# Sums of rows on TensorE, the last expert kept on chip, and products to fill a gap: one change to a transformer block with a mixture of experts

## The chip, the cores and the metric

The kernel runs on one core of one Trainium2 chip. Its time is the device time of one execution in microseconds; the median of three runs is given. TensorE (PE in the profile) multiplies matrices into PSUM, VectorE (DVE), ScalarE (ACT) and GpSimd (POOL) work on tiles of 128 partitions, and SyncE (SP) issues most of the transfers between HBM and the chip. TensorE's clock is granted by the chip; the profile shows it as a share of full speed (2.4 GHz), and its other level is half of that (1.2 GHz).

## The reference, cut to what matters

The reference is one transformer block on 1024 tokens of width 1024. After attention and a first normalization, every token is routed to 2 of 32 experts, and the results are added and normalized:

```python
t = h.reshape(B * S, D)                                   # 1024 x 1024
g_prob = softmax(t @ w_rg + b_rg)                         # 4 groups, the best one
e_top, e_idx = top_k(e_in_group, 2)                       # 2 of its 8 experts
e_w = softmax(e_top) * g_w
for e in range(32):
    hid = silu(t @ w1[e]) * (t @ w3[e])                   # 1024 -> 256
    y = y + gate[:, e:e + 1] * (hid @ w2[e])              # 256 -> 1024
...
x = layer_norm(DN_ALPHA * x + gt2[:, None, :] * f, ln2_g, ln2_b)   # f is y
```

All of it is f32.

## The kernel before, in words

The kernel does attention first; the change starts where the first normalization is done and the tokens are routed. Eight tiles of 128 tokens are taken through `products`, `residual`, `first_norm`, `second_norm`, `transposed`, `logits`, `choose` (which experts), `place` (which slot of the expert) and `slots`. VectorE does the small operations of the routing in order, tile by tile; the last tile, 7, goes through the shorter `fast_first` and `fast_second`. `slot_rows` then turns the slots into row numbers, `gather_x` fetches the first three experts' rows from HBM into `xg`, `weigh` and `slot_weights` work out the gates.

In the expert loop (`for e in range(NE)`) each expert has up to 128 slots. Its rows are transposed (`expert_x`, tile `etp`), multiplied with the gate and up weights into `eph` (`expert_up`), passed through silu and the gate (`expert_act`, tile `esg`), transposed again (`expert_h`, `ehp`) and multiplied with the down weights (`expert_down`, tile `ey`). A product of f32 values is done as three single-pass products, of high and low parts: `split` makes a weight's high part on ScalarE (`ehi`) and the low part on VectorE (`elo`). For the very first expert the low parts are held back (`hold=True`) and made later by `low_parts`. Weights come in pages of 1 MB; `page` hands the pages of three pools out in turn, and a load waits until its page has been split. `scatter_y` writes an expert's rows to `dy` in HBM by their row numbers: each token has two rows there, one for each of its experts, 1024 rows apart.

After the loop comes a branch: if some expert had more than 128 tokens (`nblk > 0`), a block for the overflow runs. It is skipped in the profiled execution. Then the last phase: for each of eight tiles of 128 tokens the two rows are loaded from `dy` (`rr`, `r2s`), added, multiplied with `gt2`, added to the kept residual `xa`, normalized and written out. Its order is written by hand in the string `LAST`: a letter is a step, a digit the tile. On TensorE a sum is made by multiplying with the identity (`summed`): a and b add the two rows, x and z add the residual. On VectorE b is an addition, g the product with `gt2`, s and o the scaling and shifting, and m a fused addition for the tiles of `FDX`. Else m, the mean, is on ScalarE, and so is most of v, the variance; v ends with two small operations on GpSimd.

The orders of TensorE, VectorE, ScalarE and GpSimd are as the code is written; each engine works its list off in order. SyncE's list is set by a scheduler.

Of the kernel before, what the change touches and what calls it, by code (L numbers as in the profile page):

```python
# [10 lines left out]
F32 = mybir.dt.float32  # L11
# [4 lines left out]
AF = mybir.ActivationFunctionType  # L16
# [30 lines left out]
FDX = (0, 7)  # L47
FPS = (3, 5)
# [36 lines left out]
x1 x2 x3 x4 b0 g0 m0 b1 v0 g1 s0 z1 b2 m1 o0 v1 a3 g2 s1 z2 b4 b3 m2 o1 v2 a5 g4 g3 z4 s2 z3 m4 b6  # L85
o2 v4 b5 g6 m3 x5 s4 v3 g5 x6 o4 z5 s3 b7 z6 m5 o3 v5 g7 m6 s5 v6 m7 o5 v7 s6 s7 o6 o7
# [72 lines left out]
def block_kernel(ctx, tc, A, out, dbg=None, stop=99):  # L159
# [1134 lines left out]
    GP.memset(ones, 1.0)  # L1294
    gat = rtp.tile([128, 2, NT], F32, name="gat")
# [45 lines left out]
    def weigh(t):  # L1341

        L, g8, m8 = (rt[t].pop(n) for n in ("L", "g8", "m8"))
        ng_ = rtw.tile([128, 4], F32, name="rng")
        V.tensor_tensor(ng_[:, 0:1], m8[:, 1:2], m8[:, 0:1], op=OP.subtract)
        V.tensor_tensor(L[:, :4], L[:, :4], g8[:, 0:1].to_broadcast([128, 4]), op=OP.subtract)
        SC.activation(L[:, :4], L[:, :4], AF.Exp, accum_out=ng_[:, 1:2])
        SC.activation(ng_[:, 0:1], ng_[:, 0:1], AF.Exp)
        V.scalar_tensor_tensor(ng_[:, 2:3], ng_[:, 0:1], 1.0, ng_[:, 1:2], op0=OP.add, op1=OP.mult)
        V.reciprocal(gat[:, 0, t:t + 1], ng_[:, 2:3])  # L1350
        V.tensor_tensor(gat[:, 1, t:t + 1], gat[:, 0, t:t + 1], ng_[:, 0:1], op=OP.mult)
# [277 lines left out]
    place(t - 2)  # L1629
    transposed(t)  # L1630
# [10 lines left out]
    slots(t)  # L1641
    keep(t, z)
# [53 lines left out]
    def expert_down(xpool, pp, W2, Hs):  # L1696
        y = xpool.tile([128, D], F32, name="ey", bufs=NEY)
        for half in range(2):
            ps = pp.tile([128, 512], F32, name="eyp", bufs=2)
            cs = slice(half * 512, half * 512 + 512)  # L1700
            for k in range(2):
                mm3(ps, Hs[0][:, k], Hs[1][:, k], *(x[:, cs] for x in W2[k]), k == 0, k == 1)
            SC.activation(y[:, cs], ps, AF.Copy)
        return y
# [61 lines left out]

    with tc.tile_pool(name="ex", bufs=2) as ex, tc.tile_pool(name="epp", bufs=1, space=PSUM) as epp:
# [3 lines left out]
        low_parts(2)  # L1771
# [4 lines left out]
        def down(e):  # L1776
            return expert_down(ex, epp, W.pop((e, 2)), Hs)
# [7 lines left out]
        for e in range(NE):  # L1785
# [25 lines left out]
        scatter(down(NE - 1), NE - 1)  # L1811
# [5 lines left out]
    with tc.If(nblk > 0):  # L1817
        with tc.tile_pool(name="otp", bufs=1, space=PSUM) as otp:
            overflow_tables(otp.tile([128, 512], F32, name="osums"))
        with tc.For_i(0, nblk) as b:  # L1820
            with tc.tile_pool(name="ow", bufs=1) as ow, tc.tile_pool(name="opp", bufs=1, space=PSUM) as opp:
                ve = nc.values_load(blk[0:1, bass.ds(b, 1)], min_val=0, max_val=NE - 1)
                Wo = [split(fetch(ve, i, pg), i) for i in range(3)]
                cols = wr[:, 7, :2].bitcast(I32)
                gc = wr[:, 7, 2:3]
                V.tensor_copy(cols[:, 0:1], gidx[:, bass.ds(b + NE, 1)])
                V.tensor_copy(cols[:, 1:2], sidx[:, bass.ds(b + NE, 1)])
                V.tensor_copy(gc, gsl[:, bass.ds(b + NE, 1)])
                gather_x(xg[0], cols[:, 0:1])
                *_, Xo = expert_x(ow, opp, xg[0])  # L1830
                ph = expert_up(opp, Wo, Xo)
                scatter_y(expert_down(ow, opp, Wo[2], expert_h(es2, opp, expert_act(es2, ph, gc))), cols[:, 1:2])


    ews.close()
    with tc.tile_pool(name="fin", bufs=NT) as fp, tc.tile_pool(name="fpp", bufs=4, space=PSUM) as fpp:
        rr, r2s = [], []
        for t in range(NT):
            for rows_, o, n in ((rr, 0, NT), (r2s, S, NT)):
                rows_.append(fp.tile([128, D], F32, name=f"fr{o}", bufs=n))  # L1840
                SY.dma_start(rows_[t], dy[o + t * 128:o + (t + 1) * 128])  # L1841
# [3 lines left out]
        def summed(t, j, x, first):  # L1845

            if first:
                fs[t, j] = fpp.tile([128, D], F32, name="fps")
            for half in range(2):
                sl = slice(half * 512, half * 512 + 512)  # L1850
                PE.matmul(fs[t, j][:, sl], ident, x[:, sl], start=first, stop=not first)  # L1851

        def added(t):
            V.tensor_tensor(rr[t], rr[t], r2s[t], op=OP.add)

        def gated(t):
            V.tensor_tensor(rr[t], fs.pop((t, 0)) if t in FPS else rr[t], gt2, op=OP.mult)

# [18 lines left out]
        def shift(t):  # L1877
# [48 lines left out]
```

## Time and profile before

| | us |
|---|---|
| median of 3 runs | 1409.38 (1406.3 to 1409.62) |
| the profiled execution | 1403.06 |
| its span, first to last instruction | 1401.3 |
| mean granted clock over the span | 0.967 |
| TensorE busy | 1308.8 (93%) |
| VectorE busy | 1145.8 (82%) |
| ScalarE busy | 717.4 (51%) |
| GpSimd busy | 440.5 (31%) |

The span is a little less than the program's time; the rest lies before the first and after the last instruction. The shares are averages over stages with different limits. The expert loop at its steady pace lies between 1055 and 1340, the last phase takes the last 57 us.

### The profile page before, as it was taken

How to read it: one execution, taken by the hardware profiler on the slowest of the kernel's cores; microseconds unless marked ns; L12 is line 12 of the kernel's file. 1: busy time of each engine (PE TensorE's matmuls, PEld its weight loads, DVE VectorE, ACT ScalarE, POOL GpSimd, SP SyncE). 2: the span in 40 equal slices, each digit the busy share in tenths (PEclk: the TensorE clock that was granted, in tenths of full speed). 3: DMA queues.
4: the chain of work that ended last, by engine and by line, in shares of the span. 5: the costliest groups of instructions: out<-in, count | busy, mean ns of one | idle time of the engine just before them, and what ended most of it. 6: DMA issues, size and time to landing. Idle time of an engine off the chain costs nothing. (4 is left out here: it accounts for less than half of the span.)

```text
span 1401.3 us, 21266 instructions
## 1 busy us (share of the span) xinstructions
PE 1308.8 (93%) x7535; PEld 1057.7 (75%) x7535; DVE 1145.8 (82%) x2137; ACT 717.4 (51%) x1306; POOL 440.5 (31%) x474
## 2 busy tenths in 40 slices
PE   4989999999999999998989999999779999999965
PEld 2568888887888788985557778999758888888832
DVE  5738888887988899974788749788889999999947
ACT  1546765444244321323665644222248888889824
POOL 2422123375237521232544425211212222222114
PEclk9999999999999999999999999999869999999987
DMA  8475422112211223103864458745469999999954
GB/s 285 158 210 183 138 78 76 43 56 73 72 61 39 74 87 106 61 31 122 318 230 138 137 152 261 273 168 209 151 214 374 372 381 371 373 348 363 375 224 177
DMA packets 133998, 264.91 MB, mean 189 GB/s; under 512 B 20736, under 2 KB 71224, under 8 KB 131840
## 3 DMA queue, kind: packets, MB, share of 16 engines
q1 hardware_dynamic: 122960, 245.40, 50.4%
q0 software_dynamic: 9216, 16.80, 3.2%
q8 instruction: 60, 0.98, 0.3%
q10 hardware_dynamic: 1712, 1.32, 0.3%
q14 instruction: 50, 0.41, 0.1%
HBM read 229.61 MB, written 50.62 MB: 200 GB/s over the span
## 5 line engine op out<-in xcount | busy, mean ns | idle before, releaser
L1554 DVE TENSOR_TENSOR elo<-pg,ehi 128x1024 fp32r<-128x1024 f32 x188 | 219.0, 1219 | 17.6 <-ACT ehi L1549 8.9
L181 PE MATMUL pj<-hTh,whi 128*128 128x512 f32 (+1 forms) x528 | 211.0, 400 | 0.0
L182 PE MATMUL pj<-hTl,whi 128*128 128x512 f32 (+1 forms) x528 | 207.1, 392 | 1.9 <-DVE hTl L307 1.2
L183 PE MATMUL pj<-hTh,wlo 128*128 128x512 f32 (+1 forms) x528 | 207.2, 392 | 0.1
L815 POOL TENSOR_TENSOR wlo<-raw,whi 128x512 fp32r<-128x512 f32 x84 | 114.5, 1378 | 289.0 <-ACT whi L814 268.8
L1549 ACT ACTIVATE ehi<-pg 128x1024 fp32r<-128x1024 f32 x192 | 190.1, 1075 | 1.0 <-PE eph L183 1.0
L517 DVE MATCH_REPLACE8 acc<-m,acc 128x1024 f32<-128x1024 f32 (+2 forms) x192 | 167.1, 878 | 0.0
L514 DVE MAX8 m<-acc 128x8 f32<-128x1024 f32 (+2 forms) x192 | 162.2, 881 | 0.0
L496 DVE SCALAR_TENSOR_TENSOR acc<-ixr,iwt,acc 128x128 f32<-128x128 f32 (+3 forms) x120 | 107.3, 933 | 23.9 <-ACT ixr L489 23.1
L181 PEld LDWEIGHTS pj<-hTh,whi 128*128 128x128 f32 (+1 forms) x528 | 98.6, 187 | 23.1 <-issue 1.7
L183 PEld LDWEIGHTS pj<-hTh,wlo 128*128 128x128 f32 (+1 forms) x528 | 98.5, 186 | 22.9 <-issue 0.6
L182 PEld LDWEIGHTS pj<-hTl,whi 128*128 128x128 f32 (+1 forms) x528 | 98.8, 187 | 22.2 <-DVE hTl L307 2.7
L181 PE MATMUL pj<-whi,hTh 128*128 128x256 f32 x384 | 111.8, 291 | 0.0
L182 PE MATMUL pj<-wlo,hTh 128*128 128x256 f32 x384 | 108.6, 283 | 0.0
L183 PE MATMUL pj<-whi,hTl 128*128 128x256 f32 x384 | 108.5, 283 | 0.0
L181 PE MATMUL eph<-ehi,xh 128*128 128x512 f32 x256 | 105.4, 412 | 0.0
L182 PE MATMUL eph<-elo,xh 128*128 128x512 f32 x256 | 102.8, 402 | 1.1 <-DVE elo L1559 1.1
L183 PE MATMUL eph<-ehi,xl 128*128 128x512 f32 x256 | 102.4, 400 | 0.0
L489 ACT ACTIVATE ixr<-ips 128x128 f32<-128x128 f32 (+7 forms) x128 | 80.7, 653 | 41.7 <-PE ips L487 32.9
L1573 POOL DMA_INDIRECT xg<-dh,gidx x32 | 34.2, 1070 | 161.4 <-PE etp L1669 139.9
L181 PEld LDWEIGHTS pj<-whi,hTh 128*128 128x128 f32 x384 | 73.4, 191 | 6.9 <-issue 5.5
L181 PE MATMUL yps<-whi,pg 128*128 128x256 f32 x256 | 76.0, 297 | 0.2 <-ACT pg L1234 0.2
(318 smaller groups left out, 3128.2 us busy)
## 6 DMA issues: line engine op xcount, KB each, us to landing
pg<-in_w_exp_gate_dram SPq DMA_DIRECT2D x64, 512.0 KB
pg<-in_w_exp_up_dram SPq DMA_DIRECT2D x64, 512.0 KB
pg<-in_w_exp_down_dram SPq DMA_DIRECT2D x32, 1024.0 KB
raw<-in_w_in_dram SPq DMA_DIRECT2D x20, 1024.0 KB
wada<-in_w_ada_dram SPq DMA_DIRECT2D x16, 1024.0 KB
dgate<-gate SPq DMA_DIRECT2D x48, 256.0 KB
gate<-dgate SPq DMA_DIRECT2D x48, 256.0 KB
wada<-in_w_ada_dram SPq DMA_DIRECT2D x16, 512.0 KB
```

The lines of the kernel that those rows point to most:

```text
L181: PE.matmul(ps, ah, bh, start=first, stop=False)
L182: PE.matmul(ps, ah, bl, start=False, stop=False)
L183: PE.matmul(ps, al, bh, start=False, stop=last)
L489: SC.activation(r, ps, AF.Relu)
L496: V.scalar_tensor_tensor(acc[i], r, sc, acc[i], op0=OP.mult, op1=OP.add)
L514: V.max(m, acc[i])
L517: V.match_replace(acc[i], m, acc[i], -3.0e38)
L815: GP.tensor_tensor(lo[:, k:k + 2], raw[:, k:k + 2], hi[:, k:k + 2].bitcast(F32), op=OP.subtract)
L1549: SC.activation(h3, src, AF.Copy)
L1554: V.tensor_tensor(*args, op=OP.subtract)
L1573: GP.indirect_dma_start(out=x, out_offset=None, in_=dh2, in_offset=bass.IndirectOffsetOnAxis(ap=gi, axis=0), bounds_check=S - 1, oob_is_er ...
```

## The change

The change has five parts.

1. The last expert's rows `y31` stay on chip. Nothing is scattered for it; instead zeros are scattered to its rows at expert 1 (`y0`). A matrix `P31` with a one where slot and token meet is built on VectorE after expert 29, and the step p of the last phase adds `P31` times `y31` to a tile's sum on TensorE.
2. The loads of the rows of the first three tiles (`NRR`) are issued before the last expert's down products, into pages, and once more within the overflow block.
3. In the last phase both rows of all tiles are added on TensorE (a and b), never on VectorE. Three tiles instead of two have the residual added on VectorE (`FDX`). `LAST` is new.
4. `busy` multiplies ones with ones into a PSUM tile that nobody reads, 20 times ahead of the transposes of tile 7 and 10 times ahead of the gate sums.
5. Two of the four held low parts are made before the first expert's rows are transposed, one of them between two halves of `weigh`.

The core of the diff:

```diff
-FDX = (0, 7)
-FPS = (3, 5)
+FDX = (0, 3, 7)
+NRR = 3
...
-x1 x2 x3 x4 b0 g0 m0 b1 v0 g1 s0 z1 b2 m1 o0 v1 a3 g2 s1 z2 b4 b3 m2 o1 v2 a5 g4 g3 z4 s2 z3 m4 b6
+p0 p2 p1 p3 a0 b0 g0 a1 m0 b1 x1 g1 v0 a2 s0 b2 z1 g2 a3 m1 o0 b3 v1 s1 p4 x2 g3 a4 m3 z2 o1 b4 m2 p5 g4 v2 a5
...
+    def busy(ps, n):
+        for _ in range(n):
+            PE.matmul(ps, ones, ones[:, None, :].to_broadcast([128, 4, 128]), start=True, stop=True)
...
     place(t - 2)
+    busy(lpp.tile([128, 512], F32, name="yps", bufs=5), 20)
     transposed(t)
...
+    busy(lpp.tile([128, 512], F32, name="yps", bufs=5), 10)
...
-        weigh(t - 1 + i)
+        weigh(t - 1 + i, (0,))
+    low_parts(1)
+    for i in range(2):
+        weigh(t - 1 + i, (1,))
     for i in range(3):
         slot_weights(t - 2 + i)
+    low_parts(1)
     V.tensor_copy(gsl[:, :NE], gps)
...
+    rr, r2s = [], []
+    def load_rows(t):
+        for rows_, o in ((rr, 0), (r2s, S)):
+            SY.dma_start(rows_[t], dy[o + t * 128:o + (t + 1) * 128])
...
-        low_parts(2)
...
+            if e == 1:
+                y0 = ex.tile([128, D], F32, name="ey", bufs=NEY)
+                GP.memset(y0, 0.0)
+                scatter(y0, NE - 1)
...
-        scatter(down(NE - 1), NE - 1)
+            if e == NE - 3:
+                own = page(pg).rearrange("p (t n) -> p t n", t=2)
+                P31, y31 = own[:, 0], own[:, 1]
+                f8 = wr[:, 7, 4:12]
+                V.tensor_copy(f8[:, 0:1], gidx[:, NE - 1:NE])
+                V.tensor_scalar(f8[:, 1:NT], pid[:, 0, 1:NT], pid[:, 0, 0:1], None, op0=OP.subtract)
+                V.scalar_tensor_tensor(f8[:, 1:NT], f8[:, 1:NT], -1.0, f8[:, 0:1].to_broadcast([128, NT - 1]),
+                                       op0=OP.mult, op1=OP.add)
+                for t in range(NT):
+                    V.tensor_scalar(P31[:, t * 128:(t + 1) * 128], iota, f8[:, t:t + 1], None, op0=OP.is_equal)
+        for t in range(NRR):
+            a = page(pg).rearrange("p (t n) -> p t n", t=2)
+            rr.append(a[:, 0])
+            r2s.append(a[:, 1])
+            load_rows(t)
+        down(NE - 1, y31)
...
     order.close()
...
-                Wo = [split(fetch(ve, i, pg), i) for i in range(3)]
+                Wo = [split(fetch(ve, i, pages[1]), i) for i in range(3)]
...
+        for t in range(NRR):
+            load_rows(t)
...
+        def summed(t, j, x, first, last, w=None):
+            ps = tile_of(t, j)
             for half in range(2):
                 sl = slice(half * 512, half * 512 + 512)
-                PE.matmul(fs[t, j][:, sl], ident, x[:, sl], start=first, stop=not first)
-        def added(t):
-            V.tensor_tensor(rr[t], rr[t], r2s[t], op=OP.add)
+                PE.matmul(ps[:, sl], ident if w is None else w, x[:, sl], start=first, stop=last)
         def gated(t):
-            V.tensor_tensor(rr[t], fs.pop((t, 0)) if t in FPS else rr[t], gt2, op=OP.mult)
+            V.tensor_tensor(rr[t], fs.pop((t, 0)), gt2, op=OP.mult)
...
-            "a": lambda t: summed(t, 0, rr[t], True),
-            "b": lambda t: summed(t, 0, r2s[t], False) if t in FPS else added(t),
+            "p": lambda t: summed(t, 0, y31, True, False, P31[:, t * 128:(t + 1) * 128]),
+            "a": lambda t: summed(t, 0, rr[t], False, False),
+            "b": lambda t: summed(t, 0, r2s[t], False, True),
             "g": gated,
-            "x": lambda t: summed(t, 1, xa[t], True),
-            "z": lambda t: summed(t, 1, rr[t], False),
+            "x": lambda t: summed(t, 1, xa[t], True, False),
+            "z": lambda t: summed(t, 1, rr[t], False, True),
```

Where it moves instructions, the orders of the engines show what stands where. The first place is TensorE in the last phase. `fps` is the PSUM tile of a sum; `pg_138..`/`pg_139..` are the pages of the residual, `fr0` and `fr1024` the two rows of a tile. Before, the 16 rows of this phase have two instructions each; the first twelve:

```order
L1851 MATMUL fps_14523<-pg_13893,ident_65 128x512 x2
L1851 MATMUL fps_14526<-pg_13895,ident_65 128x512 x2
L1851 MATMUL fps_14529<-pg_13895,ident_65 128x512 x2
L1851 MATMUL fps_14532<-pg_13897,ident_65 128x512 x2
L1851 MATMUL fps_14523<-fr0_14492,ident_65 128x512 x2
L1851 MATMUL fps_14557<-fr0_14500,ident_65 128x512 x2
L1851 MATMUL fps_14526<-fr0_14496,ident_65 128x512 x2
L1851 MATMUL fps_14557<-fr1024_14502,ident_65 128x512 x2
L1851 MATMUL fps_14575<-fr0_14508,ident_65 128x512 x2
L1851 MATMUL fps_14532<-fr0_14504,ident_65 128x512 x2
L1851 MATMUL fps_14529<-fr0_14500,ident_65 128x512 x2
L1851 MATMUL fps_14575<-fr1024_14510,ident_65 128x512 x2
```

Now there are 31 rows with 68 instructions, of which the first twelve are these (`pg_14038` holds `P31` and `y31`, `pg_14208`, `pg_14211` and `pg_14214` the rows of the first three tiles, `pg_13930` the residual):

```order
L1897 MATMUL fps_14571<-pg_14038 128x512 x2
L1897 MATMUL fps_14574<-pg_14038 128x512 x2
L1897 MATMUL fps_14577<-pg_14038 128x512 x2
L1897 MATMUL fps_14580<-pg_14038 128x512 x2
L1897 MATMUL fps_14571<-pg_14208,ident_65 128x512 x4
L1897 MATMUL fps_14577<-pg_14211,ident_65 128x512 x4
L1897 MATMUL fps_14594<-pg_13930,ident_65 128x512 x2
L1897 MATMUL fps_14574<-pg_14214,ident_65 128x512 x4
L1897 MATMUL fps_14594<-pg_14211,ident_65 128x512 x2
L1897 MATMUL fps_14580<-fr0_14548,ident_65 128x512 x2
L1897 MATMUL fps_14580<-fr1024_14549,ident_65 128x512 x2
L1897 MATMUL fps_14623<-pg_14038 128x512 x2
```

Ahead stood four residual tiles that wait for no row of `dy`; now there stand four selections of the last expert's rows, and from the fifth row on each sum waits for a load.

The second place is SyncE between the last loads of the expert loop and the rows of the last phase, with what each instruction waits for (a name such as DMAHW3 is the count of a ring of transfers that SyncE uses in turn, DMASW one of GpSimd's). Before, the skip of the overflow block and the first loads:

```order
L1810 DMA pg_13902<-dada_595 128x1024 [waits DMAHW6_49]
...
L1817 UNCONDITIONAL_BRANCH [waits SP_sequencer_49,DMAHW0_49,DMAHW1_49,DMAHW2_49,DMAHW3_49,DMAHW7_49]
L1841 DMA fr0_14488<-dy_8559 128x1024 [waits DMASW2_49,DMASW3_49,DMASW1_49,DMASW4_49,DMASW0_49,DMASW5_49,DVE_49,DMASW7_49,PE_49,DMAHW7_49,Activation_49,Pool_49]
L1841 DMA fr1024_14490<-dy_8559 128x1024 [waits DMAHW0_49]
L1841 DMA fr0_14492<-dy_8559 128x1024 [waits DMAHW1_49]
```

Now the first six loads, the skip and the next load:

```order
L1834 DMA pg_13939<-dada_595 128x1024 [waits DMAHW6_49]
L1785 DMA pg_14208<-dy_8559 128x1024 [waits DMAHW7_49,DMASW7_49,DVE_49]
L1785 DMA pg_14208<-dy_8559 128x1024 [waits DMAHW0_49]
L1785 DMA pg_14211<-dy_8559 128x1024 [waits DMAHW1_49,DVE_49]
L1785 DMA pg_14211<-dy_8559 128x1024 [waits DMAHW2_49]
L1785 DMA pg_14214<-dy_8559 128x1024 [waits DMAHW3_49,DVE_49]
L1785 DMA pg_14214<-dy_8559 128x1024 [waits DMAHW4_49]
...
L1857 UNCONDITIONAL_BRANCH [waits SP_sequencer_49,DMAHW0_49,DMAHW1_49,DMAHW2_49,DMAHW3_49,DMAHW4_49,DMAHW5_49,DMAHW6_49,DMAHW7_49]
L1785 DMA fr0_14548<-dy_8559 128x1024 [waits DMASW1_49,DVE_49,DMAHW0_49,PE_49,Activation_49]
```

Six of the 16 loads have moved ahead of the branch, and the branch's row on the path that skips the block waits for eight rings instead of five. The first sums of rows on TensorE now wait for these rings (a0, b0, a1, b1):

```order
L1897 MATMUL fps_14571<-pg_14208,ident_65 128x512 [waits DMAHW7_49,DMAHW2_49]
...
L1897 MATMUL fps_14571<-pg_14208,ident_65 128x512 [waits DMAHW3_49,DMAHW0_49]
...
L1897 MATMUL fps_14577<-pg_14211,ident_65 128x512 [waits DMAHW4_49,DMAHW1_49]
...
L1897 MATMUL fps_14577<-pg_14211,ident_65 128x512 [waits DMAHW5_49]
...
L1897 MATMUL fps_14574<-pg_14214,ident_65 128x512 [waits DMAHW6_49]
```

Each of the first three waits for two rings: for that of its load and for one that the skipped block would have used.

The third place is VectorE at the hand-over from routing to the first expert. `rng`, `rL` and `gat` belong to `weigh`, `rEg` to `slot_weights`, `elo` are the held low parts, `xl` the low part of the first expert's rows. Before:

```order
L1345 TENSOR_TENSOR rng<-rm_10714 128x1
L1346 TENSOR_TENSOR rL<-rL,rg_10705 128x4
L1349 SCALAR_TENSOR_TENSOR rng<-rng 128x1
L1350 RECIPROCAL gat<-rng 128x1
L1351 TENSOR_TENSOR gat<-gat,rng 128x1
L1379 TENSOR_SCALAR rEg<-jp,exf,gat 128x32 x6
L1650 COPY gsl<-gps 128x32
L1652 COPY cnt<-sums 128x32
L1671 TENSOR_TENSOR xl<-etp,xh 128x512
L1559 TENSOR_TENSOR elo_10612<-pg,ehi_10611 128x1024
L1671 TENSOR_TENSOR xl<-etp,xh 128x512
L1559 TENSOR_TENSOR elo_10615<-pg,ehi_10614 128x1024
```

Now:

```order
L1351 TENSOR_TENSOR rng<-rm_10735 128x1
L1352 TENSOR_TENSOR rL<-rL,rg_10726 128x4
L1567 TENSOR_TENSOR elo_10612<-pg,ehi_10611 128x1024
L1357 SCALAR_TENSOR_TENSOR rng<-rng 128x1
L1358 RECIPROCAL gat<-rng 128x1
L1359 TENSOR_TENSOR gat<-gat,rng 128x1
L1357 SCALAR_TENSOR_TENSOR rng<-rng 128x1
L1358 RECIPROCAL gat<-rng 128x1
L1359 TENSOR_TENSOR gat<-gat,rng 128x1
L1387 TENSOR_SCALAR rEg<-jp,exf,gat 128x32 x6
L1567 TENSOR_TENSOR elo_10615<-pg,ehi_10614 128x1024
L1664 COPY gsl<-gps 128x32
```

Two of the four `elo` that followed `xl` stand ahead of it now, one where VectorE waited for ScalarE.

## Rows read from the trace of the kernel before

**Rows 1.** The page: granted clock in 40 equal slices of the span, in tenths

```profile
PEclk9999999999999999999999999999869999999987
```

**Rows 2.** Windows, expert loop (stretch, its length, each engine's busy us, clock, DMA share, GB/s)

```profile
1055.00:1340.00 285.00, 284.91 (x1377) 234.23 (x1375) 262.80 (x296) 247.94 (x357) 58.76 (x56) 1.00 0.96 361
```

**Rows 3.** Timeline, last phase (start, us, engine, line, what, count, idle before)

```profile
1340.60 0.97 POOL L1707 DMA_INDIRECT dy<-ey,sidx  x1 [7.47 <-ACT ehh L1692]
...
1344.63 0.97 POOL L1707 DMA_INDIRECT dy<-ey,sidx  x1 [3.05 <-ACT ey L1703]
...
1344.89 7.13 PE L1851 MATMUL fps<-pg,ident 128*128 128x512 f32 x16 [1.17 <-ACTq L1817]
...
1348.67 13.39 SPq L1841 DMA_DIRECT2D fr<-dy  x16
...
1353.66 1.23 DVE L1854 TENSOR_TENSOR fr<-fr,fr 128x1024 f32<-128x1024 f32 x1 [12.60 <-DMA fr<-dy]
...
1359.92 3.75 PE L1851 MATMUL fps<-fr,ident 128*128 128x512 f32 x4 [7.90 <-POOL fst L1871]
...
1382.38 3.60 PE L1851 MATMUL fps<-fr,ident 128*128 128x512 f32 x8
...
1395.12 1.42 DVE L1882 SCALAR_TENSOR_TENSOR fr<-fr,fst,pg 128x512 f32<-128x512 f32 x2 [0.44 <-POOL fst L1872]
```

**Rows 4.** Groups of instructions, last phase (count, busy us, mean ns, idle before)

```profile
L1854 DVE TENSOR_TENSOR fr<-fr,fr 128x1024 f32<-128x1024 f32 x6 | 7.3, 1220 | 12.6 <-DMA fr<-dy 12.6
...
L1875 DVE SCALAR_TENSOR_TENSOR fr<-fr,fst,pg 128x1024 f32<-128x1024 f32 x8 | 10.2, 1280 | 2.4 <-ACT fj L1870 2.4
```

**Rows 5.** Windows, hand-over from routing to the experts

```profile
1010.00:1030.00 20.00, 10.53 (x49) 9.73 (x50) 14.62 (x79) 4.81 (x11) 4.80 (x5) 0.50 0.24 84
...
1044.20:1048.00 3.80, 3.79 (x11) 3.02 (x12) 3.80 (x6) 3.28 (x5) 0.43 (x1) 0.55 0.97 337
```

**Rows 6.** Timeline, hand-over

```profile
1022.00 0.47 DVE L1369 TENSOR_SCALAR rP<-jp,psf 128x128 fp32r<-128x128 f32 x2
...
1024.51 0.16 DVE L1349 SCALAR_TENSOR_TENSOR rng<-rng 128x1 f32<-128x1 f32 x1 [0.46 <-ACT rng L1348]
...
1029.63 1.97 PE L1669 MATMUL etp<-ident,xg 128*128 128x128 f32 x8 [0.35 <-DVE cnt L1652]
...
1031.46 0.69 DVE L1671 TENSOR_TENSOR xl<-etp,xh 128x512 fp32r<-128x512 f32 x1 [1.89 <-ACT xh L1670]
...
1033.81 3.49 DVE L1559 TENSOR_TENSOR elo<-pg,ehi 128x1024 fp32r<-128x1024 f32 x3
...
1038.23 0.39 PE L182 MATMUL eph<-elo,xh 128*128 128x512 f32 x1
...
1038.46 0.40 PE L183 MATMUL eph<-ehi,xl 128*128 128x512 f32 x1
...
1040.79 1.05 PE L1669 MATMUL etp<-ident,xg 128*128 128x128 f32 x8
...
1043.69 0.46 DVE L1683 SCALAR_TENSOR_TENSOR esg<-esg,gsl,eph 128x256 f32<-128x256 f32 x1
...
1044.20 0.44 PE L1689 MATMUL ehp<-ident,esg 128*128 128x128 f32 x2 [2.36 <-DVE esg L1683]
```

**Rows 7.** Windows, last phase

```profile
1348.60:1356.40 7.80, 3.42 (x8) 1.16 (x7) 2.67 (x3) 0.00 (x0) 0.00 (x0) 0.92 0.83 295
...
1348.60:1358.10 9.50, 3.42 (x8) 1.16 (x7) 4.37 (x5) 0.41 (x2) 0.00 (x0) 0.85 0.87 318
...
1359.90:1368.40 8.50, 7.28 (x8) 2.67 (x9) 6.62 (x6) 2.56 (x5) 3.39 (x3) 0.50 1.03 414
...
1368.40:1386.00 17.60, 17.57 (x41) 7.55 (x39) 16.32 (x15) 9.20 (x19) 6.94 (x7) 0.99 0.45 183
```

**Rows 8.** Line 1817, the branch: SyncE's waits (count, ns, first and last start)

```profile
L1817 SPq EVENT_SEMAPHORE  x6: 17/17/17, 1324.6 to 1334.4; - x6
```

**Rows 9.** Waits of TensorE, routing and first experts (us in total, times, longest)

```profile
PE yps L1519 <- DVE lx L1507: 5.9, 1, 5.9
```

More of the change, by code (lines that the diff above doesn't have):

```diff
@@ L84 @@
 LAST = """
-x1 x2 x3 x4 b0 g0 m0 b1 v0 g1 s0 z1 b2 m1 o0 v1 a3 g2 s1 z2 b4 b3 m2 o1 v2 a5 g4 g3 z4 s2 z3 m4 b6
-o2 v4 b5 g6 m3 x5 s4 v3 g5 x6 o4 z5 s3 b7 z6 m5 o3 v5 g7 m6 s5 v6 m7 o5 v7 s6 s7 o6 o7
+p0 p2 p1 p3 a0 b0 g0 a1 m0 b1 x1 g1 v0 a2 s0 b2 z1 g2 a3 m1 o0 b3 v1 s1 p4 x2 g3 a4 m3 z2 o1 b4 m2 p5 g4 v2 a5
+s2 x4 v3 s3 b5 z4 g5 p6 m4 o2 x5 v4 o3 a6 p7 s4 b6 z5 g6 a7 m5 o4 x6 v5 s5 b7 z6 g7 m6 m7 v6 o5 v7 s6 s7 o6 o7
 """
@@ L1339, in choose, with weigh @@
         V.scalar_tensor_tensor(Mb[:, t], iota[:, :NE], exf[:, 1, t:t + 1], M1, op0=OP.is_equal, op1=OP.add)
[L1341 to L1351, printed above, removed]
+    def weigh(t, parts=(0, 1)):
+        L, g8, m8 = (rt[t][n] for n in ("L", "g8", "m8"))
+        if 0 in parts:
+            ng_ = rt[t]["ng"] = rtw.tile([128, 4], F32, name="rng")
+            V.tensor_tensor(ng_[:, 0:1], m8[:, 1:2], m8[:, 0:1], op=OP.subtract)
+            V.tensor_tensor(L[:, :4], L[:, :4], g8[:, 0:1].to_broadcast([128, 4]), op=OP.subtract)
+            SC.activation(L[:, :4], L[:, :4], AF.Exp, accum_out=ng_[:, 1:2])
+            SC.activation(ng_[:, 0:1], ng_[:, 0:1], AF.Exp)
+        if 1 in parts:
+            ng_ = rt[t]["ng"]
+            V.scalar_tensor_tensor(ng_[:, 2:3], ng_[:, 0:1], 1.0, ng_[:, 1:2], op0=OP.add, op1=OP.mult)
+            V.reciprocal(gat[:, 0, t:t + 1], ng_[:, 2:3])
+            V.tensor_tensor(gat[:, 1, t:t + 1], gat[:, 0, t:t + 1], ng_[:, 0:1], op=OP.mult)
     def place(t):
@@ L1694, in expert_h, with expert_down @@
         return hh, hl
-    def expert_down(xpool, pp, W2, Hs):
-        y = xpool.tile([128, D], F32, name="ey", bufs=NEY)
+    def expert_down(xpool, pp, W2, Hs, y=None):
+        y = xpool.tile([128, D], F32, name="ey", bufs=NEY) if y is None else y
         for half in range(2):
@@ L1774, in block_kernel, with down @@
         count_blocks()
-        def down(e):
-            return expert_down(ex, epp, W.pop((e, 2)), Hs)
+        def down(e, y=None):
+            return expert_down(ex, epp, W.pop((e, 2)), Hs, y)
         def scatter(y, e):
@@ L1832, in block_kernel @@
                 scatter_y(expert_down(ow, opp, Wo[2], expert_h(es2, opp, expert_act(es2, ph, gc))), cols[:, 1:2])
+        for t in range(NRR):
+            load_rows(t)
     ews.close()
     with tc.tile_pool(name="fin", bufs=NT) as fp, tc.tile_pool(name="fpp", bufs=4, space=PSUM) as fpp:
[L1837 to L1841, printed above, removed]
+        for t in range(NRR, NT):
+            for rows_, o in ((rr, 0), (r2s, S)):
+                rows_.append(fp.tile([128, D], F32, name=f"fr{o}", bufs=NT - NRR))
+            load_rows(t)
         fs = {}
@@ L1844, in block_kernel, with tile_of @@
         s_, m_, q_, r_ = (st[:, i] for i in range(4))
-        def summed(t, j, x, first):
-            if first:
+        def tile_of(t, j):
+            if (t, j) not in fs:
                 fs[t, j] = fpp.tile([128, D], F32, name="fps")
+            return fs[t, j]
+        def summed(t, j, x, first, last, w=None):
+            ps = tile_of(t, j)
             for half in range(2):
                 sl = slice(half * 512, half * 512 + 512)
-                PE.matmul(fs[t, j][:, sl], ident, x[:, sl], start=first, stop=not first)
-        def added(t):
-            V.tensor_tensor(rr[t], rr[t], r2s[t], op=OP.add)
+                PE.matmul(ps[:, sl], ident if w is None else w, x[:, sl], start=first, stop=last)
         def gated(t):
-            V.tensor_tensor(rr[t], fs.pop((t, 0)) if t in FPS else rr[t], gt2, op=OP.mult)
+            V.tensor_tensor(rr[t], fs.pop((t, 0)), gt2, op=OP.mult)
         def mean(t):
```

## The prediction

> **What bounds the kernel now.** I read the slices of the page first, then the windows, then the timeline of two stretches, the routing and the last phase. In the slices [rows 1] the granted clock leaves full speed only twice: where routing hands over to the experts, and at the end. Between them lies the expert loop: TensorE is busy 284.91 of 285 us there at the full clock [rows 2], so nothing the change adds on other engines in that stretch counts unless it makes TensorE wait, and a head start that the loop gets is kept to its end.
>
> The last phase runs from the last expert's products to the end at 1401.3. In its timeline [rows 3] the scatter of the last expert is issued at 1344.63, SyncE begins to load rows at 1348.67, VectorE gets the first pair at 1353.66, and TensorE, which had x1 to x4 to do from 1344.89 to 1352.0, sits idle until 1359.92. From 1353.66 on it is mostly VectorE that sets the pace: its operations of 128x1024 take 1.22 to 1.28 us [rows 4], and 32 of them fill most of the 42.9 us until its last one ends at 1396.54 [rows 3].
>
> In the hand-over the clock is at half (1.2 GHz) from 1010 to 1030 [rows 5], and TensorE's last wait there is for VectorE: `ehp` of the first expert starts at 1044.20 after 2.36 us of waiting for `esg`, which VectorE does after a chain from 1031.46 on [rows 6].
>
> **The price of a sum on TensorE.** This decides the case. A sum of 128x1024 on TensorE is two matmul instructions of 128x512 in f32. The timeline shows x1 to x4, eight instructions in the order's listing, as 16 records in 7.13 us [rows 3]: each f32 product is two records. The pitch is 0.429 us a record (41 records in 17.57 us at the full clock [rows 7]), so an instruction costs 0.858 us and a sum 1.72 us. A single-pass product of the same shape has a pitch of 0.23 us [rows 6]. At half clock the four records of z1 took 3.75 us [rows 3].
>
> The Trainium skill (FP8 and Floating Point Precision, section Matmul Precision) says that a true FP32 product takes four passes through the array. By four single passes of 0.23 us an instruction would cost 0.93 and the last phase some 5 us more than I count below; the trace's own records are shorter, and I go by them.
>
> **The change, part by part: the last phase.** The steps of the list are now p, a and b for all eight tiles, x and z for five: 34 sums, 68 instructions, against 16 sums before. TensorE needs 34 x 1.716 = 58.3 us at the full clock, against 27.5. VectorE loses six adds (7.3 us [rows 4]) and one z and x become a third fused add: 27 operations instead of 32, about 33 us. So TensorE becomes the bound of this phase, by 25 us.
>
> When does it start? p needs the last expert's y on chip, which is there when the scatter was issued before, so p0 starts where x1 did, at 1344.89, and p0 to p3 fill TensorE until 1351.8. The first rows: their loads now wait for the scatter of the expert before the last, issued at 1340.60. The last scatter took from 1344.63 until the loads at 1348.67, so by the same 4.0 us the loads start at about 1344.6, 4 us sooner. From the first issue on, 2.30 MB were moved in 7.8 us and 3.02 MB in 9.5 [rows 7]; six loads of 0.52 MB each are 3.15 MB, landed 9.8 us after the first issue, at 1354.4, the first four at about 1351.8, the fifth at about 1353.
>
> Here the order shows a wait that the diff doesn't: on the path that skips the overflow block SyncE raises the counts of rings that the block would have used, and must wait for what is in flight on them. Before, those were five rings and the waits were over at 1334.4 [rows 8]. Now the block holds six loads more, the row of SyncE's branch lists all eight rings, and a0 waits for rings 7 and 2, b0 for 3 and 0, a1 for 4 and 1: so a0 starts only when the first four loads have landed (1351.8), b0 after the fifth (TensorE gets to it at 1353.5), a1 after all six (1354.4, TensorE gets to it at 1355.2). Taken in turn TensorE waits about 0.3 us there. If the loads landed as late as 13 us after their issue it would be 3 us; below nothing is excluded, as TensorE is not idle before. The other ten loads are issued behind that wait, at 1354.5, and a3, the first to need them, comes at 1365.5.
>
> After z6, the last sum, the end is as before: z6's records ended at 1382.38 + 3.60 = 1385.98, the span at 1401.3, 15.3 us later, of which some 0.4 were ScalarE still at another tile [rows 3]. I take 15.0.
>
> So the new end, with no head start, is 1344.89 + 58.3 + 0.3 + 15.0 = 1418.5 instead of 1401.3: 17.2 us later. VectorE's saving of 6 us and the earlier loads are hidden under TensorE.
>
> **The hand-over.** Two of the four held low parts move ahead of the chain that ends in `esg`, at 3.49 / 3 = 1.16 us each: 2.3 us out of it. They take the place of two waits of 0.46 us for ScalarE (the one at 1024.51 and its like) and of VectorE's wait for the gate sums, so that the transposes of the first expert start at about 1029.3 instead of 1029.63. With the clock up they take 1.05 us, as the next expert's do, not 1.97 [rows 6], and the first half is ready 0.5 us sooner. So `xl` starts 0.9 us earlier and `esg` 0.9 + 2.3 = 3.2 us earlier. TensorE's own work (24 products at 0.23 us from 1030.5) would be done by 1037, so VectorE stays the last to come, and the gain is 3.2 us.
>
> Does the clock get there? Twenty products whose results nobody reads come where TensorE waited 5.9 us for tile 7 [rows 9], ten where it waits for the gates. The trace has no product of bf16 and 512 columns; the nearest row is the single-pass one, 0.23 us, twice that at half clock. So the twenty take 4.6 to 9.2 us and the ten 2.3 to 4.6. At worst, all at half clock, the twenty hold the transposes of tile 7 up by 9.2 - 5.9 = 3.3 us, which eats the gain; at best the low clock of 1044.2 to 1048 [rows 5] goes too, where 3.8 us of TensorE's work at a mean clock of 0.55 would take 2.1, worth 1.7 us. I keep 0 and 4.9 us as ends and take 3.2: products that start at half clock can end at full, as the first expert's own did (half clock until 1030, 0.23 us a product at 1038 [rows 5, 6]).
>
> **The rest.** The memset and the scatter of zeros for the last expert at e = 1 stand where GpSimd is busy 58.8 of 285 us [rows 2], and the number of scatters is unchanged. The selection matrix adds eight 128x128 selects, 0.24 us each [rows 6], and three small operations, 2.4 us, to VectorE in the 30th expert; VectorE idles 22 of 285 us [rows 2], and the two experts left have no weights to prepare behind them: 0, at most 0.5 us. SyncE's load of the block count now stands in the middle of the weight loads, behind work that is ready by then: 0.
>
> **Sum.** 17.2 - 3.2 = 14.0 us on the profiled execution's 1403.06 (span 1401.3), which lies 6.3 us under the median of the runs, 1409.38. I add the difference to the median: 1423.4.
>
> **Rivals.**
> 1. The clock falls while TensorE waits for the first rows. Before, TensorE went idle at 1352.0 and was at half speed from 1359.92 to 1368.4 [rows 7]. Had it to wait 3 us from 1351.8 for a0, and ran at half clock for the first two sums, it would lose 3 + 4 us: 1430. Against it: the wait comes out at 0.3 us, with p0 to p3 just before.
> 2. The other side, faster: a sum costs half of what I take, that is the 16 records are 16 instructions. Then TensorE has 29 us to do, less than VectorE's 33, and VectorE is the bound: first g0 at 1355, 27 operations of 1.2 us and waits of some 4 us as before, ending at 1391 instead of 1396.5; with the head start 8.7 us less, 1400.7. The point from which it decides: a sum under 0.97 us (33 us over 34 sums). For it speaks that a single-pass product of this shape takes 0.23 us; against it that eight listed instructions left 16 records in 7.13 us [rows 3].
> 3. The hand-over gives nothing, because the unread products get in the way of the chain as much as they lift the clock: 1409.4 + 17.2 = 1426.6. For it: TensorE's waits there are for VectorE, not for the clock.
>
> **How the numbers follow.** The forecast 0.78 (1421 to 1428 as its own range: head start of 1 to 4.9 us, wait of 0 to 3), rival 1 0.08, rival 2 0.05, rival 3 0.06, others 0.03. Cases 1, 3 and the forecast are slower by more than 0.3% (4.2 us, about what a measurement of this kernel tells from no change): 0.92, faster 0.05, within it 0.03. The runs before spread over 3.3 us, and from the profiled execution instead of the median the sum is 1417.1; with both the range is 1414 (1417.1 - 3.3) to 1431 (1428 + 3), which leaves out rival 2 and little else.
>
> **What would show it.** Right: `fps` has 136 records at a pitch of 0.43 us, TensorE is busy without a pause from the first p to z6, some 58 us, and VectorE's g's wait for it 3 to 5 us each; a0 starts within 1 us of p3's end; `ehp` of the first expert starts at about 1041. Wrong: one record per sum instruction, VectorE without waits in the last phase, a granted clock of half in the last phase, or `esg` later than 1042.

## The result, and the profile after

The changed kernel takes 1420.91 us (median of 10 runs, 1412.98 to 1423.23), the kernel before on the same chips 1404.04 (10 runs, 1399.07 to 1409.62): 1.2% slower, ratio 1.0120 (95% interval 1.0097 to 1.0142). Profiled against profiled execution it is 1419.38 against 1403.06, 16.3 us more. The forecast was 14.0 us more, and 1423.4 us for the median.

Four stretches make up the 16.3 us; the change acts in the last three. I measure them from one point that both kernels have, VectorE's operation `rng` of tile 5 (1001.26 before, 999.93 after), since the stages ahead of it differ by a microsecond or more from run to run.

| us | before | after | difference |
|---|---|---|---|
| start of the span to `rng` | 1001.26 | 999.93 | -1.3 (nothing changed there) |
| `rng` to the first expert's `ehp` | 42.94 | 40.29 | -2.65 |
| `ehp` to the first sum (x1 or p0) | 300.69 | 299.17 | -1.5 |
| first sum to the end of the span | 56.4 | 78.2 | +21.8 |

The hand-over first, in the timeline (start, duration, engine, line, operation, count, idle time before and what ended it), and the window behind `ehp` (length, busy time of each engine, granted clock, DMA share, GB/s). They answer [rows 5, 6].

```profile
1028.35 1.13 PE L1683 MATMUL etp<-ident,xg 128*128 128x128 f32 x8 [1.14 <-DMA xg<-dh,gidx]
...
1039.70 0.46 DVE L1697 SCALAR_TENSOR_TENSOR esg<-esg,gsl,eph 128x256 f32<-128x256 f32 x1
...
1040.22 0.44 PE L1703 MATMUL ehp<-ident,esg 128*128 128x128 f32 x2 [2.34 <-DVE esg L1697]
```

```profile
1040.22:1044.02 3.80, 3.80 (x18) 3.07 (x19) 3.80 (x6) 3.54 (x6) 0.42 (x1) 1.00 1.01 379
```

`ehp` still waits for `esg`, 2.34 us against 2.36, so VectorE is still what comes last, only sooner. The transposes `etp` now wait 1.14 us for the gather of the rows, no longer for VectorE, so a shorter list of VectorE would not start them sooner. Behind `ehp` the clock is at full speed where it was 0.55.

The last phase, in the timeline; these rows answer [rows 3].

```profile
1335.09 0.98 POOL L1721 DMA_INDIRECT dy<-ey,sidx  x1 [6.16 <-ACT ehh L1706]
...
1339.39 7.13 PE L1897 MATMUL fps<-pg 128*128 128x512 f32 x16 [1.18 <-ACTq L1857]
...
1341.87 3.36 SPq L1785 DMA_DIRECT2D pg<-dy  x6
```

```profile
1350.41 15.58 PE L1897 MATMUL fps<-pg,ident 128*128 128x512 f32 x32 [3.89 <-SPq L1857]
...
1400.15 3.60 PE L1897 MATMUL fps<-fr,ident 128*128 128x512 f32 x8
```

```profile
1355.78 1.23 DVE L1900 TENSOR_TENSOR pg<-fps,pg 128x1024 f32<-128x1024 f32 x1 [20.23 <-PE fps L1897]
...
1395.20 1.23 DVE L1900 TENSOR_TENSOR fr<-fps,pg 128x1024 f32<-128x1024 f32 x1 [4.65 <-PE fps L1897]
...
1411.44 1.41 DVE L1925 SCALAR_TENSOR_TENSOR fr<-fr,fst,pg 128x512 f32<-128x512 f32 x2 [0.72 <-POOL fst L1915]
```

And its groups of instructions (count, busy time, mean ns, idle time before), with two windows:

```profile
L1897 PE MATMUL fps<-pg,ident 128*128 128x512 f32 x52 | 25.0, 627 | 3.9 <-SPq L1857 3.9
L1897 PE MATMUL fps<-fr,ident 128*128 128x512 f32 x52 | 23.6, 592 | 0.0
L1897 PE MATMUL fps<-pg 128*128 128x512 f32 x32 | 14.7, 595 | 1.2 <-ACTq L1857 1.2
...
L1900 DVE TENSOR_TENSOR fr<-fps,pg 128x1024 f32<-128x1024 f32 x5 | 6.1, 1223 | 13.6 <-PE fps L1897 13.6
```

```profile
1356.00:1404.00 48.00, 47.75 (x112) 20.85 (x110) 26.02 (x24) 13.33 (x27) 9.30 (x12) 1.00 0.38 153
```

```profile
1350.00:1354.00 4.00, 3.59 (x5) 1.71 (x6) 0.00 (x0) 0.00 (x0) 0.00 (x0) 0.57 0.38 155
```

There are 52 + 52 + 32 = 136 records for 68 instructions. From 1356 to 1404 TensorE is busy 47.75 of 48 us, and the five later of VectorE's eight products with `gt2` wait for it 13.6 us in all, the longest 4.65 us. But TensorE also stood idle for 3.89 us before a0, which waited for SyncE at the skipped branch, and worked at a clock of 0.57 just behind. From p0 to the end of z6 there are 1400.15 + 3.60 - 1339.39 = 64.4 us; 58.3 are the sums, 3.9 the idle time, and most of the other 2.2 the half clock.

### The profile page after: what moved, and what is told of

Same layout as the page of the kernel before. It is cut to its first block, busy times and chain, and to the rows that moved or that the text cites. A ratio compares the mean times of both kernels' runs of the same rounds, so it can differ in the third digit from the quotient of the medians.

```text
span 1417.6 us, 21466 instructions
## 1 busy us (share of the span) xinstructions
PE 1337.0 (94%) x7637; PEld 1066.7 (75%) x7637; DVE 1141.0 (80%) x2144; ACT 715.7 (50%) x1304; POOL 446.5 (32%) x475
```

## The experiments

A run's time depends on the stages ahead by several microseconds (the first sum stands anywhere from 1337.4 to 1348.3 in these traces), so where a few microseconds matter I go by stretches of the trace. The whole times don't tell the changed kernel, e2, e6, e9 and e10 apart (their intervals overlap); what is said of the differences among these rests on one trace of each.

| kernel | ratio to before (95%) | `rng` to `ehp` | `rng` to first sum | first sum to end |
|---|---|---|---|---|
| before | 1 | 42.94 | 343.6 | 56.4 |
| after | 1.0120 (1.0097 to 1.0142) | 40.29 | 339.5 | 78.2 |
| e1 hand-over alone | 0.9971 (0.9946 to 0.9997) | 40.50 | 339.7 | 56.6 |
| e2 last phase alone | 1.0141 (1.0108 to 1.0175) | 42.95 | 343.7 | 74.2 |
| e3 low parts alone | 0.9972 (0.9953 to 0.9991) | 40.94 | 340.1 | 56.4 |
| e4 unread products alone | 0.9986 (0.9962 to 1.0010) | 42.09 | 343.5 | 56.6 |
| e5 sums in one pass | 0.9951 (0.9925 to 0.9977) | 40.67 | 339.8 | 52.7 |
| e6 no loads in the skipped block | 1.0087 (1.0061 to 1.0113) | 40.63 | 339.9 | 72.5 |
| e7 sums on TensorE alone | 1.0082 (1.0058 to 1.0105) | 42.97 | 343.7 | 67.7 |
| e8 hand-over, x4 repeated | 0.9942 (0.9923 to 0.9962) | 40.34 | 339.5 | 53.1 |
| e9 no broadcasts | 1.0123 (1.0088 to 1.0158) | 40.69 | 339.9 | 77.0 |
| e10 half of the residual's loads | 1.0109 (1.0089 to 1.0130) | 40.48 | 339.6 | 72.9 |

(In e7 TensorE has no sum ahead of the rows; its last two numbers are counted to and from where x1 stood before, 0.26 us behind the issue of the last scatter.)

**Which part does what: e1 to e4.** My theory was that the hand-over gives what the trace shows and the last phase costs the rest; the rival, that the head start is drift and nothing comes of it. e1 is the kernel before with parts 4 and 5, e2 the changed kernel without them, e3 and e4 the kernel before with one of the two:

```diff
     place(t - 2)
+    busy(lpp.tile([128, 512], F32, name="yps", bufs=5), 20)     # e1, e4; taken out in e2
     transposed(t)
...
-        weigh(t - 1 + i)
+        weigh(t - 1 + i, (0,))                                  # e1, e3; undone in e2
+    low_parts(1)
```

> The kernel before with parts 4 and 5 of the change alone (unread products, two low parts earlier); its last phase is untouched. My theory: the first expert's esg comes about 2.7 us earlier, the clock is full behind it and gives 1.5 us more, and the expert loop keeps both: 4.2 us faster than before (ratio 0.997). Rival, the head start in the changed kernel was drift of the stages ahead: within 1 us of before.

> The changed kernel without parts 4 and 5: the last expert's rows on chip, the sums on TensorE, the earlier loads alone. My theory: the last phase costs 21.8 us and nothing gives it back: 1404 + 21.8 = 1426 (ratio 1.0155). Rival, the hand-over gives nothing: the same time as the changed kernel, 1421 (1.012).

> The kernel before with the two low parts moved and no unread products. My theory: VectorE's chain to esg is shorter by 2.3 us, and the clock stays at half for the first expert: 2 to 3 us faster than before, ehp about 2.5 us earlier against the same point of the routing, half clock behind it as before. Rival (the clock does it all): no gain, since the first expert's products at half clock come last.

> The kernel before with the unread products and no low parts moved. My theory: esg still comes at the end of the same chain on VectorE, ehp at most 1 us earlier; what is left is the clock behind it, 1.5 us: 1 to 2.5 us faster than before. Rival (the clock does it all): 4 us faster.

The rows that decide, e3 (low parts) and then e4 (unread products), each with the window behind `ehp`:

```profile
1041.79 0.44 PE L1696 MATMUL ehp<-ident,esg 128*128 128x128 f32 x2 [2.59 <-DVE esg L1690]
```

```profile
1041.80:1045.60 3.80, 3.80 (x18) 3.08 (x19) 3.80 (x6) 3.34 (x5) 0.41 (x1) 1.00 0.96 350
```

```profile
1046.97 0.69 PE L1696 MATMUL ehp<-ident,esg 128*128 128x128 f32 x2 [4.02 <-DVE esg L1690]
```

```profile
1046.90:1050.70 3.80, 3.73 (x10) 3.05 (x11) 3.80 (x7) 2.71 (x4) 0.49 (x1) 0.50 0.99 362
```

The low parts alone bring the first sum 3.55 us sooner, the unread products alone 0.2, both together 4.0 (e1). The rival that the clock does it all has fallen: in e4 the clock is up earlier and the first expert's products are done earlier, but TensorE then waits 4.02 us for `esg` instead of 2.36, and behind that wait the clock is 0.50 for 3.8 us. What it gains ahead of `ehp` (0.85 us) it loses behind (0.67). In e3, without any unread product, the clock behind `ehp` is full. In all eight traces with the low parts moved the first sum stands 299.1 to 299.3 us behind `ehp`, before and in e2 300.7: the 1.5 us go with the low parts. So e1 met the forecast. e3 did in part: `ehp` came 2.0 us sooner, about as expected, but I had expected half clock behind it and 2 to 3 us in all. e4 gave less than I had put (1 to 2.5 us). e2 was a miss: I expected 1426, it took 1421.05, the same as the changed kernel with its head start. Its last phase takes 74.2 us and not 78.2. From `rng` to the end it is 343.7 + 74.2 = 417.9 us, against 339.5 + 78.2 = 417.7 in the changed kernel. So 4 us of the last phase go with the hand-over, and the head start had been given back somewhere: that is what e6, e9 and e10 look for.

```profile
1339.81 0.97 POOL L1707 DMA_INDIRECT dy<-ey,sidx  x1 [6.27 <-ACT ehh L1692]
...
1343.90 3.33 SPq L1771 DMA_DIRECT2D pg<-dy  x5
```

```profile
1352.68 14.00 PE L1884 MATMUL fps<-pg,ident 128*128 128x512 f32 x32 [1.45 <-SPq L1844]
```

Without the hand-over the six loads start 4.1 us behind the scatter of expert 30, as I had forecast, not 6.8, and a0 waits 1.45 us.

**The price of a sum: e5 and e7.** The rival here was that the wait for the first rows and the clock cost the time.

```diff
-                PE.matmul(ps[:, sl], ident if w is None else w, x[:, sl], start=first, stop=last)
+                PE.matmul(ps[:, sl], (ident if w is None else w).bitcast(BF)[:, 1::2], x[:, sl].bitcast(BF)[:, 1::2],
+                          start=first, stop=last)                                   # e5, on the changed kernel
...
-FPS = (3, 5)
+FPS = (0, 1, 2, 3, 4, 5, 6, 7)                                                       # e7, on the kernel before,
+a0 b0 g0 a1 m0 b1 x1 g1 v0 a2 s0 b2 z1 g2 a3 m1 o0 b3 v1 s1 x2 ...                   # LAST of the change without p
```

> The changed kernel whose last-phase sums read only the upper halves of their numbers (bf16, one pass); the output is that of rounded rows. Same order, same waits. My theory, the price of a sum bounds the last phase: 34 sums at about 0.46 us are 16 us, VectorE becomes the bound, and the phase from the first p to the end takes 52 to 57 us instead of 78.2; time 20 us under the changed kernel, 1396 to 1402. Rival (the wait for the first rows and the clock cost the time): the phase keeps at least 70 us, time 1412 or more.

> The kernel before with one part alone: both rows of all tiles added on TensorE, in the changed kernel's order and with its three fused tiles, but without the last expert's rows on chip (no p) and with before's loads. My theory: 26 sums, 44.6 us of TensorE behind the first rows at about 8.8 us, plus 14 us behind the last sum: 67.5 us from the end of the experts, 2 to 4 more for half clock after the long wait; time 11 to 15 us over before. Rival (the sums are not what costs): at most 3 us over before.

e5, the first p, the first two g on VectorE and the last operation, then e7's first and last sums:

```profile
1341.08 1.97 PE L1897 MATMUL fps<-pg 128*128 128x512 bf16 x7 [1.18 <-ACTq L1857]
1351.46 1.01 PE L1897 MATMUL fps<-pg,ident 128*128 128x512 bf16 x2 [8.40 <-SPq L1857]
```

```profile
1353.86 1.23 DVE L1901 TENSOR_TENSOR pg<-fps,pg 128x1024 f32<-128x1024 f32 x1 [16.62 <-PE fps L1897]
...
1387.64 1.42 DVE L1926 SCALAR_TENSOR_TENSOR fr<-fr,fst,pg 128x512 f32<-128x512 f32 x2 [0.71 <-POOL fst L1916]
```

```profile
1354.47 8.74 PE L1851 MATMUL fps<-fr,ident 128*128 128x512 f32 x16 [8.49 <-DMA fr<-dy]
...
1397.38 3.60 PE L1851 MATMUL fps<-fr,ident 128*128 128x512 f32 x8
```

With a quarter of the price the same order takes 52.7 us instead of 78.2, although TensorE waits even longer for its first rows (8.40 us) and starts at half clock. A single pass is one record of about 0.22 us. The Trainium skill (FP8 and Floating Point Precision, section Matmul Precision) has four passes for a true FP32 product; an f32 instruction of 0.858 us is about four times the single pass here. VectorE is the bound then, and its 27 operations without the wait for sums would beat the kernel before by 3.7 us in this phase: the order is sound, the price of f32 sums is not. e7 shows it from the other side: with no rows kept on chip and no early loads, the sums in the new order, with three fused tiles, cost 67.7 - 56.4 = 11.3 us (forecast 11 to 15).

**Where the head start went: e6, e9 and e10.** In the changed kernel a0 waits for SyncE. Two causes were open: the rings of the skipped block, and the late start of the six loads.

```diff
-        for t in range(NRR):                                    # e6: the loads at the end of the overflow block
-            load_rows(t)
...
-                    SY.dma_start(gb[:, j], A[src][0:1].to_broadcast([128, D]))
+                    SY.dma_start(gb[:, j], dx1[j * 128:(j + 1) * 128])              # e9, and gt2 likewise
...
-                for _ in range(FX0):
+                for _ in range(2):                              # e10
                     load_xa(SY)
+                xa.extend(xa)
```

> The changed kernel without the second set of loads inside the overflow block, which is skipped (the rows of the first three tiles would lack the overflow, of which there is none). My theory: SyncE's skip then waits for fewer rings, a0 follows p3 within 1 us of its two loads' landing, TensorE's idle time of 3.9 us goes to 0 to 2 and the clock stays up: the last phase takes 73 to 75 us, 3 to 5 us less than in the changed kernel's trace, 0 to 2 less than in the trace without the hand-over (74.2). Rival, the loads themselves land late: no change, 74 to 78.

> The changed kernel whose three broadcast loads (the gain, the bias and gt2, one row to 128 partitions) read 128 different rows of the residual's buffer instead: same bytes, same order, other numbers in the output. Theory: in the changed kernel the scatter of expert 30 waited on one transfer engine that was still at these broadcasts for 18 us after the last one's issue, so that the head start of the hand-over was lost there. Then the row loads start 4.1 us after the scatter's issue instead of 6.8, TensorE's idle time ahead of a0 falls from 3.9 to about 1.4 us with the clock up, and the phase from the first p takes 74 us instead of 78.2: 4 us faster than the changed kernel, 1417. Rival (the scatter itself is slower there, or the residual's loads hold it up): loads 6.5 to 7 us after the scatter, phase 76 to 78, no change.

> The changed kernel with half of the residual's loads left out (2 of 4 MB; tiles 4 to 7 add the residual of tiles 0 to 3, other numbers in the output). The broadcasts are as they were. Theory: the first row loads start when the slowest transfer engine has drained what was issued ahead, 18 us after the last of these loads in all runs with the hand-over; with 2 MB less in the queues it drains some 5 us earlier, behind the scatter of expert 30: the row loads start about 4.1 us after the scatter's issue, TensorE's idle time ahead of a0 is 1 to 1.5 us, the phase from the first p takes 73.5 to 74.5 us. Rival (the drain is a fixed delay behind the last load, or the scatter's own): loads 5.8 to 7 us after the scatter, phase 76 to 78.

Each with the scatter of expert 30, SyncE's loads and a0; e6 first:

```profile
1341.58 0.97 POOL L1721 DMA_INDIRECT dy<-ey,sidx  x1 [5.62 <-ACT ehh L1706]
...
1348.57 1.46 SPq L1785 DMA_DIRECT2D pg<-dy  x3
```

```profile
1352.96 13.90 PE L1895 MATMUL fps<-pg,ident 128*128 128x512 f32 x32
```

Then e9 and its window just ahead of the loads:

```profile
1342.43 0.98 POOL L1721 DMA_INDIRECT dy<-ey,sidx  x1 [6.27 <-ACT ehh L1706]
...
1348.26 1.93 SPq L1785 DMA_DIRECT2D pg<-dy  x4
```

```profile
1356.40 15.70 PE L1897 MATMUL fps<-pg,ident 128*128 128x512 f32 x32 [2.54 <-SPq L1857]
```

```profile
1347.00:1348.00 1.00, 1.00 (x3) 0.40 (x3) 0.00 (x0) 0.00 (x0) 0.00 (x0) 1.00 0.07 25
```

And e10:

```profile
1342.42 0.97 POOL L1721 DMA_INDIRECT dy<-ey,sidx  x1 [6.27 <-ACT ehh L1706]
...
1346.20 3.31 SPq L1785 DMA_DIRECT2D pg<-dy  x6
```

```profile
1354.04 14.00 PE L1898 MATMUL fps<-pg,ident 128*128 128x512 f32 x32 [0.18 <-SPq L1858]
```

```profile
1342.00:1343.00 1.00, 0.53 (x2) 0.37 (x3) 0.88 (x2) 0.42 (x2) 0.58 (x1) 1.00 0.00 0
```

In e6 the loads start as late as 7.0 us behind the scatter, and yet a0 follows p3 without a pause: it waits for no more than its own two loads, which have landed by 4.4 us after the first issue. With the loads in the block a0 comes 7.8 to 8.8 us after the first issue (the changed kernel, e2, e5, e9, e10). So the rings of the skipped block are what turns a late start into idle time.

The late start itself: before the loads, the DMA share falls to 0.06 or 0.07, one engine of 16. In the changed kernel they go out 18.5 us after SyncE's last load of the loop was issued (1323.38 to 1341.87). e9 says that the broadcasts are not the cause, against my theory: with other rows loaded, and as many bytes, the engine is still at work (0.07) and the loads start 5.8 us behind the scatter. In e10, with 2 MB less ahead, nothing is in flight just after the scatter is issued (0.00), the loads start 3.8 us behind it, and a0 waits 0.18 us. That doesn't show that the amount counts by itself: SyncE's queue ends 17.7 us behind its last load in e10 as in the changed kernel, and 16.8 to 18.3 us in all twelve traces; but in e10 that load goes out 18.3 us ahead of the scatter, in the changed kernel 11.7.

What the one engine does stands in the DMA queues, where q0 has GpSimd's transfers and q1 SyncE's (a packet is a piece of a transfer; the lines have packets, MB, share of 16 engines): first the last loads of the changed kernel and of e10, then the queues of the changed kernel from 1340.00 to 1341.00 and of e6 from 1348.10 to 1348.60.

```profile
1323.38 1.04 SPq L1834 DMA_DIRECT2D pg<-dada  x1
```

```profile
1324.10 1.09 SPq L1835 DMA_DIRECT2D pg<-dada  x1
```

```profile
q0 software_dynamic: 3, 0.01, 3.0%
q1 hardware_dynamic: 3, 0.01, 3.0%
```

```profile
q1 hardware_dynamic: 3, 0.01, 6.0%
```

The engine takes packets of the scatter and of SyncE's loads in turn, one of 4 KB each, at 0.16 us a packet. So expert 30's scatter is late because its own last packets share that engine with loads given earlier: in the changed kernel its last packet ends at 1341.3 and the row loads follow 0.5 us later, as they follow the end of the scatter's packets by 0.4 to 0.6 us in all twelve traces (in those that scatter the last expert too, the end of that scatter's packets). They don't wait for SyncE's backlog to end: in e6 the scatter's packets end at 1348.1, the loads go out at 1348.57, and packets of the earlier loads go on until 1348.7. The Trainium skill has a rule that bears on this (DMA: Bandwidth & Descriptors, section Queues, rings and completion order): an engine's increment of a semaphore lands only after its earlier writes, across queues. The traces neither need it nor speak against it, since every earlier packet on that engine was done when the scatter's own last one ended. The result is 3.8 to 4.1 us from issue to completion where SyncE's queue had ended when the scatter's packets began, against 5.8 to 7.0. Why it is one engine that lags is open.

The head start makes that collision: SyncE's last load is issued at 1323.38 in the changed kernel and 1323.11 in e2, but p0 stands at 1339.39 and 1344.10. The hand-over moved TensorE, not the transfers. Counted from `rng`, p0 came 4.2 us sooner than in e2 but the row loads only 1.5 us and a0 1.8 us, and the half clock behind the longer wait (15.58 us for 32 records against 14.00) took 1.6 of that.

**A version that beats both: e8.** Before's last phase loses time to the clock: TensorE is idle from x4 to z1 [rows 3, 7], and z1 and the sums behind it run at half speed. e8 is e1, with x4 made four times more and not read:

```diff
-x1 x2 x3 x4 b0 g0 m0 b1 v0
+x1 x2 x3 u4 u4 u4 u4 x4 b0 g0 m0 b1 v0
...
+            "u": lambda t: summed(t, 1, xa[t], True, True),
```

> The kernel with the hand-over changes and before's last phase, in which x4 is made four times more into its own PSUM tile and not read, so that TensorE works on while it waits for the first rows. My theory: the clock stays full, z1 and the sums behind it take half as long, and VectorE's waits for them (1.89 and 0.92 us) go: the last phase takes 54 us instead of 56.6, time 6 to 7 us under before (ratio 0.995). Rival, VectorE is the bound and the sums at half clock lie beside it: 56.6 us, the same as with the hand-over alone.

```profile
1341.64 14.00 PE L1864 MATMUL fps<-pg,ident 128*128 128x512 f32 x32 [1.18 <-ACTq L1830]
1356.58 1.96 PE L1864 MATMUL fps<-fr,ident 128*128 128x512 f32 x4 [0.95 <-POOL fst L1884]
```

```profile
1350.33 1.23 DVE L1867 TENSOR_TENSOR fr<-fr,fr 128x1024 f32<-128x1024 f32 x1 [12.54 <-DMA fr<-dy]
...
1388.58 1.41 DVE L1895 SCALAR_TENSOR_TENSOR fr<-fr,fst,pg 128x512 f32<-128x512 f32 x2 [0.44 <-POOL fst L1885]
```

z1 takes 1.96 us instead of 3.75, the phase 53.1 instead of 56.6, a little more than the two waits I had counted. VectorE then works from 1350.33 to 1390.0 with 1.3 us of waits in all, so it is the bound. The whole is 0.58% faster than before (ratio 0.9942) and 1.8% faster than the changed kernel by the two ratios.

## Why the prediction was right, point by point

- **The price of a sum** held: 136 records, 0.429 us each, TensorE without a pause from a0 on. e5 and e7 show that this price, and not the wait, makes most of the loss; the wait and the half clock behind it add 5.6 us.
- **The hand-over** was put at 3.2 us with 4.9 as its upper end. It is 2.65 us up to `ehp` and 1.5 more behind it from the clock, 4.2. The second was the end that I kept and did not take. The reason was partly wrong: it is the moved low parts that bring the clock up, not the unread products (e3, e4).
- **The first rows** were the step that failed: "their loads now wait for the scatter of the expert before the last [...] by the same 4.0 us the loads start at about 1344.6". The same 4.0 us was the duration of a scatter with empty queues. Here it was 6.8 us, since one transfer engine still had SyncE's earlier loads to move beside the scatter's packets (the queues above; e10 has 3.8 us without them). So the loads went out 2.5 us behind p0 and not 0.3 us ahead of it. A smaller part is the term for the landing: the prediction had a0 ready 7.2 us after the first issue, and it started 8.5 us after. With the rings, which the prediction had from the order, that made 3.9 us of idle time instead of 0.3, and about 1.7 at half clock. By the prediction's own signs, a0 within 1 us of p3's end and no half clock in the last phase, this part was wrong.
- So **rival 1**, which I gave 0.08, came true in its mechanism, at 5.6 us instead of 7. The total still came out within 2.3 us, between profiled executions, because three other terms were off the other way: the head start 1.0 us larger, 13.9 us behind z6 instead of 15.0, and stages ahead of the change 1.3 us shorter in this execution. That they cancel is luck. So is how near 1423.4 lies to the measured 1420.91: its base, the median of three runs (1409.38), stands 5.3 us above that of ten (1404.04), and the difference of the medians, 16.9 us, 2.9 above the 14.0.
- **Rival 2** (a sum at half the price) is excluded by the count of records. e5, at a quarter of the price, shows that its reasoning was right: cheap sums would have made the phase faster than before. **Rival 3** is excluded by e1 in the trace, though in the changed kernel's time it looks true: e2, without the hand-over, is no slower, since the last phase gave the head start back.
- The last phase was put at 17.2 + 56.4 = 73.6 us from p0; it took 78.2 in the changed kernel, 74.2 in e2, 72.5 and 72.9 in e6 and e10, where no wait for rows is left.

## What to carry to other kernels

Before work moves to an idle engine, price it at its own data type: a f32 sum on TensorE costs 1.72 us against 1.22 us of VectorE's add, and each one here sat on the engine that then set the end. A head start on one engine is worth what the transfers can follow, and a transfer that is wanted sooner shares the transfer engines with what they were given before. Here unread products helped where work on the path followed the wait (e8), and not where the next wait swallowed the gain (e4).

## What the runs showed of the hardware

- One f32 product of 512 columns is two records of 0.429 us; the same in bf16 is one of about 0.22.
- A scatter (two of them moved 0.44 MB between 1325 and 1360) is over 3.8 to 4.1 us after its issue where SyncE's queue has ended when its packets begin, and 5.8 to 7.0 us with a backlog of loads, of which the last 2 to 3 us are one engine of 16 (DMA share 0.06 to 0.07) that takes packets of both queues in turn, 0.16 us each.
- The path that skips a block waits for loads in flight on the rings that the block would have used: a0 came 7.8 to 8.8 us after the first load was issued, and by 4.4 us without those loads in the block (e6).
- TensorE's clock fell behind a wait of 4.02 us in e4 (to 0.50) and 2.36 us before (0.55), and stayed full behind 2.34 us in the changed kernel, 2.59 us in e3: the length of the wait alone does not decide. What else does, these runs leave open.
